# A fourth part by seven products in ten quads, and split first tiles at two stage starts, in an fp32 decoder layer on one core

## The chip, the core and the metric

The kernel runs on one core of a Trainium2 chip. Its metric is the device time of one execution in microseconds, weights in HBM at the start and the result in HBM at the end. Four engines work beside each other, each through its own list of instructions: TensorE (PE in the profile) multiplies, VectorE (DVE) and ScalarE (ACT) work elementwise, SyncE's queue (SP) issues the loads. Two elementwise engines prepare what TensorE multiplies, and semaphores make one engine wait for another.

## The reference

One layer with 256 tokens of width 2048, all in fp32 (shortened):

```python
x = x + 0.5 * swiglu(rms_norm(x, g1), w_gate1, w_up1, w_down1)     # FFN1, 2048 -> 5632 -> 2048
h = rms_norm(x, g_mix); p = h @ w_in                                # 2048 -> 5120: mixing
x = x + concat(diff_attention(q, k, v), conv_group(c_val, c_gate)) @ w_out
x = x + cross_attention(rms_norm(x, g_x), rms_norm(mem, g_mem))     # 256 memory tokens
x = x + 0.5 * swiglu(rms_norm(x, g2), w_gate2, w_up2, w_down2)      # FFN2
# swiglu(h, g, u, d) = (silu(h @ g) * (h @ u)) @ d
```

Three quarters of the time go into the two FFNs.

## The kernel before

**Splitting.** TensorE multiplies fp32 numbers in a shorter format (fp32r). So each weight tile `raw` is split in two: ACT casts it to `wh`, VectorE subtracts, `wl = raw - wh` (`split`). The activations stand turned, as `h` and `l` (`xh`, `xl`; `hth`, `htl` for the hidden layer). A product takes three matmuls of 128x128 by 512: `h*wh + h*wl + l*wh`.

**Quads.** An FFN goes through the 5632 hidden columns in 11 groups of 512, c = 0 to 10. For each, a *quad* (`quad`) computes gate and up for both token halves, four accumulators `acc[tb][j]` in PSUM (tb: token half; j: gate or up). After the groups 0 to 3, 4 to 7 and 8 to 10 two down quads follow, which add half their result to x. The weights of a quad come in 8 *parts*, one for each pair of row tiles. A plain part is 8 products, 24 matmuls, and two splits of 1024 elements per partition. A *seven* computes the same 2x2 block product by seven products instead of eight, in Winograd's way: sums of weight tiles (lines 241, 243, 244, on VectorE), sums of the tokens (`token_sums`, once per pair), 21 matmuls, and splits of 1024, 512, 1024, 1024. Some of the seven products go into tiles of their own (`q`: p1, q6, q57); after the last seven `middle` combines them (`us`, `vw`, `ys`), and at the quad's end `evac` adds the accumulators to these (lines 442), takes silu and multiplies (`h`, line 447). `S_IN` says which of the 8 pairs are sevens, `ORDER_IN` in which order the parts come; `ORDER_1` is that of FFN2's first quad, `ORDER_0` that of FFN1's first, which has no sevens.

**Order of the work.** A scheduler of the framework places the instructions of every engine; an engine goes through its list in order. The weights run through 3 buffers for `raw` and 7 each for `wh` and `wl`, so VectorE can be some parts ahead of TensorE and no more. The four accumulators have one buffer each: a quad's first matmul into one waits until the quad before it was evacuated. `later(n, fn)` postpones small work by n parts, above all the transposes of a finished tile (`turn`, 8 transposes) and the row sums.

**Stage starts.** Mixing (`proj` on `w_in`, columns 8 and 6 first) and FFN2 take x as FFN1 and cross attention leave it. x is normed by scaling behind the multiplication, so transposes of x can start at once; `after_x` sets them.

Of the kernel before, what the change touches and what calls it, by code (L numbers as in the profile page):

```python
# [52 lines left out]
def hybrid_layer(ctx, tc, x, head, xT, mem, memT, pos, convw, bvec, w):  # L53
# [16 lines left out]
    def later(steps, fn):  # L70
        waiting.append([steps, fn])
# [126 lines left out]

    def quad(parts, srcs, middle, evac, first=False):

# [4 lines left out]

        acc = [[accp.tile([P, 512], F32, tag=f"acc{tb}{j}", name=f"acc{tb}{j}") for j in range(2)]
               for tb in range(2)]
        begun = set()
# [87 lines left out]
    def token_sums(pool, bufs, o0, e0, o1, e1):  # L296
# [92 lines left out]
    class LazyStats:  # L389
        def __init__(self, norm):  # L390
            self.norm = norm

        def __len__(self):
            return KD

        def __getitem__(self, k):
            h, l = self.norm.grp[k // 4] if self.norm.grp[k // 4] else (None, None)
            return (h, l, k % 4, k)

    def after_x(norm, tb, n):  # L400

        norm.sq(tb, n)
        if tb == 1:
            later((1, 2, 2, 3)[n], lambda: norm.turn(n))
            if n == 3:
                later(3, norm.finish)


    def ffn(norm, wg, wu, wd, groups, done):
        with tc.tile_pool(name="wf", bufs=SPLITS, reuse_waits="tile") as wf, \  # L410
# [8 lines left out]
            for gi, ng in enumerate(groups):  # L419
                hts, hsums, hold = {}, {}, {}  # L420
                s_down = S_DOWN[ng]
                for c in range(c0, c0 + ng):
                    hts[c] = (hp.tile([P, 4, 256], F32R, tag="hth", name="hth"),
                              hp.tile([P, 4, 256], F32R, tag="htl", name="htl"))
                    start = norm is n1 and c == 0
                    sevens = () if start else S_IN
                    order = ORDER_0 if start else ORDER_1 if c == 0 else ORDER_IN
                    rest = {}
# [8 lines left out]
                    def evac(tb, acc, c=c, rest=rest, end=(c == c0 + ng - 1), pairs=(c - c0 < s_down)):  # L437
# [12 lines left out]
                        def turn():  # L450
# [15 lines left out]
                        later(2 if end else 8, turn)  # L466

                    quad(norm.parts(order, sevens),
                         [wg[:, c * 512:(c + 1) * 512], wu[:, c * 512:(c + 1) * 512]], middle, evac, first=start)
                final = gi == len(groups) - 1  # L470
                for n0 in (0, 2):
                    def middle(q, n0=n0):
# [6 lines left out]
                    def evac(tb, acc, n0=n0):  # L479
                        for j in range(2):  # L480
# [97 lines left out]
    def constants_b():  # L578
# [106 lines left out]

    w_in, w_out, w_kv = w["w_in"], w["w_out"], w["xattn_w_kv"]

    def wcols(wt, c):
        return wt[:, c * 512:(c + 1) * 512]

    n3 = Norm(G_XATT, "xa")
    with tc.tile_pool(name="mix", bufs=1, reuse_waits="tile") as mp:
        uT = [mp.tile([P, 4, 30 + 256], F32, name=f"uT{c}") for c in range(2)]
        y = mp.tile([P, 8, 256], F32, name="y")
        vt = [[mp.tile([P, 512], F32, name=f"v{tb}{c}") for c in range(2)] for tb in range(2)]
        for c in range(2):
# [4 lines left out]
        for c in range(2):  # L701
            def evac(tb, acc, c=c):
# [413 lines left out]
```

## Time and profile before

| | us |
|---|---|
| Median of 3 runs (lowest, highest) | 1873.14 (1871.94, 1873.90) |
| Profiled execution, its own time | 1874.74 |
| Its span on the core | 1871.8 |
| Mean granted clock of TensorE, share of 2.4 GHz | 0.998 |
| TensorE busy in the span | 1852.2 |
| VectorE busy in the span | 1676.7 |

The profiled execution is one of its own, 1.6 us above the median; all durations come from it. The time beside the span (2.9 us) lies before and after the instructions. A busy TensorE is one with a matmul in its pipe; how fast they follow one another is read from their starts.

### The profile page before, as it was taken

Reading aid. Unit: us, or ns where it says so; the run is one execution under the profiler, and the core shown is the slowest. Engines: PE = TensorE matmul, PEld = TensorE weight load, DVE = VectorE, ACT = ScalarE, POOL = GpSimd, SP = SyncE. Lnnn points to the kernel's source line nnn. Section 1 sums busy time; section 2 is a strip of 40 time slices with the busy share of each in tenths; the row PEclk is TensorE's granted clock in tenths of the full one; section 3 lists DMA queues with packets and bytes.
Section 4 is the critical chain, followed back from the end, with each engine's and each line's share of the span. In section 5 each row is a group of like instructions: output and inputs, shape, how many; then the busy total and the mean of one; then the engine's idle time right before and its main releaser. Section 6 shows DMA issues by size and latency. Waiting matters only on the chain.

```text
span 1871.8 us, 23348 instructions
## 1 busy us (share of the span) xinstructions
PE 1852.2 (99%) x8365; PEld 1524.5 (81%) x8365; DVE 1676.7 (90%) x2240; ACT 1090.6 (58%) x1470; POOL 21.7 (1%) x29
## 2 busy tenths in 40 slices
PE   9999999999999999999999999999999999999998
PEld 6878888888888887888778887888888888888887
DVE  7899999999999996799997666999999999999998
ACT  7565555565545665554577656665655556555553
POOL 0000000000000000000011000000000000000000
PEclk9999999999999999999999999999999999999999
DMA  9556556656665546766644751556655666546554
GB/s 336 199 193 203 180 176 214 212 187 200 205 222 181 202 158 209 230 206 198 178 134 129 256 182 57 203 180 215 207 191 197 227 212 203 191 157 225 186 201 153
DMA packets 188756, 364.72 MB, mean 195 GB/s; under 512 B 11616, under 2 KB 12128, under 8 KB 188640
## 3 DMA queue, kind: packets, MB, share of 16 engines
q1 hardware_dynamic: 188640, 363.23, 58.6%
q8 instruction: 65, 1.06, 0.2%
q14 instruction: 51, 0.42, 0.1%
HBM read 361.09 MB, written 2.10 MB: 194 GB/s over the span
## 4 chain that ended last, share of the span: by engine, by line
PE 71%; DVE 19%; DMA 3%; issue 3%; ACT 3%; POOL 0%; SPq 0%; DVEq 0%; ACTq 0%
PE acc L277 13%; PE acc L281 13%; PE acc L279 13%; DVE wl L146 8%; DVE y L917 4%; PE acc L182 4%; PE acc L181 4%; PE acc L184 4%; PE acc L196 3%; PE q L196 3%; PE q L197 3%; PE acc L197 3%; PE q L195 3%; PE acc L195 3%; DMA raw<-ffn_w_up 2%
## 5 line engine op out<-in xcount | busy, mean ns | idle before, releaser
L145 ACT CAST wh<-raw 128x1024 fp32r<-128x1024 f32 (+1 forms) x864 | 838.3, 1001 | 664.2 <-DVE raw L241 267.0
L146 DVE TENSOR_TENSOR wl<-raw,wh 128x1024 fp32r<-128x1024 f32 (+1 forms) x864 | 975.9, 1158 | 139.6 <-ACT wh L145 124.2
L277 PE MATMUL acc<-wh,xh_f 128*128 128x512 f32 x904 | 352.7, 393 | 6.5 <-ACT wh L145 3.6
L279 PE MATMUL acc<-wl,xh_f 128*128 128x512 f32 x904 | 351.6, 391 | 0.0
L281 PE MATMUL acc<-wh,xl_f 128*128 128x512 f32 x904 | 294.4, 390 | 0.0
L277 PEld LDWEIGHTS acc<-wh,xh_f 128*128 128x128 f32 x904 | 169.7, 188 | 45.9 <-ACT wh L145 6.0
L279 PEld LDWEIGHTS acc<-wl,xh_f 128*128 128x128 f32 x904 | 170.1, 188 | 36.5 <-DVE wl L146 2.0
L281 PEld LDWEIGHTS acc<-wh,xl_f 128*128 128x128 f32 x904 | 170.0, 188 | 35.5
L277 PE MATMUL acc<-wh,hth 128*128 128x512 f32 x448 | 174.7, 392 | 0.7 <-DVE vw L442 0.4
L279 PE MATMUL acc<-wl,hth 128*128 128x512 f32 x448 | 174.5, 390 | 0.0
L281 PE MATMUL acc<-wh,htl 128*128 128x512 f32 x448 | 147.9, 390 | 0.0
L181 PE MATMUL acc<-wh,xh_mix 128*128 128x512 f32 x320 | 125.6, 394 | 1.8 <-ACT wh L145 1.8
L182 PE MATMUL acc<-wl,xh_mix 128*128 128x512 f32 x320 | 125.3, 392 | 0.5 <-DVE wl L146 0.5
L241 DVE TENSOR_TENSOR raw<-raw 128x1024 f32<-128x1024 f32 x95 | 115.5, 1216 | 0.0
L196 PE MATMUL q<-wl,sh 128*128 128x512 f32 x285 | 110.9, 389 | 0.0
L197 PE MATMUL q<-wh,sl 128*128 128x512 f32 x285 | 110.9, 389 | 0.0
L195 PE MATMUL q<-wh,sh 128*128 128x512 f32 x285 | 110.9, 389 | 0.0
L184 PE MATMUL acc<-wh,xl_mix 128*128 128x512 f32 x320 | 102.9, 391 | 0.0
L917 DVE SCALAR_TENSOR_TENSOR y<-uT,cw,y 128x256 f32<-128x256 f32 x240 | 100.4, 470 | 0.1
L277 PEld LDWEIGHTS acc<-wh,hth 128*128 128x128 f32 x448 | 84.1, 188 | 19.7 <-DVE vw L442 1.3
L281 PEld LDWEIGHTS acc<-wh,htl 128*128 128x128 f32 x448 | 84.1, 188 | 17.6
L279 PEld LDWEIGHTS acc<-wl,hth 128*128 128x128 f32 x448 | 84.2, 188 | 16.9
(299 smaller groups left out, 2502.7 us busy)
## 6 DMA issues: line engine op xcount, KB each, us to landing
raw<-ffn_w_down SPq DMA_DIRECT2D x176, 512.0 KB, 4.8
raw<-ffn_w_gate SPq DMA_DIRECT2D x175, 512.0 KB, 4.0
raw<-ffn_w_up SPq DMA_DIRECT2D x175, 512.0 KB, 5.2
raw<-w_in SPq DMA_DIRECT2D x80, 512.0 KB, 4.4
raw<-w_out SPq DMA_DIRECT2D x32, 512.0 KB, 4.8
raw<-xattn_w_kv SPq DMA_DIRECT2D x16, 512.0 KB, 3.9
raw<-xattn_w_q SPq DMA_DIRECT2D x8, 512.0 KB, 4.3
raw<-xattn_w_o SPq DMA_DIRECT2D x8, 512.0 KB, 3.8
```

What stands on the lines that cost most here:

```text
L145: last[:] = [S.copy(out=wh, in_=raw), V.tensor_tensor(out=wl, in0=raw, in1=wh.bitcast(F32), op=ALU.subtract)]
L146: V.tensor_tensor(out=wl, in0=raw, in1=wh.bitcast(F32), op=ALU.subtract)]
L181: T.matmul(acc[tb][j], hs, wt[k, j][0], start=(fresh and k == 0), stop=False)
L182: T.matmul(acc[tb][j], hs, wt[k, j][1], start=False, stop=False)
L184: T.matmul(acc[tb][j], ls, wt[k, j][0], start=False, stop=(ending and k == nk - 1))
L195: T.matmul(acc, hs, w[0], start=start, stop=False)
L196: T.matmul(acc, hs, w[1], start=False, stop=False)
L197: T.matmul(acc, ls, w[0], start=False, stop=stop)
L277: T.matmul(acc[tb][j], hs, wt[b][j][0], start=f"{tb}{j}" not in begun, stop=False)
L279: T.matmul(acc[tb][j], hs, wt[b][j][1], start=False, stop=False)
L281: T.matmul(acc[tb][j], ls, wt[b][j][0], start=False, stop=(ending and b == 1))
L917: V.scalar_tensor_tensor(out=yc, in0=u[:, j:j + 256], scalar=cw[:, j * 8 + ct:j * 8 + ct + 1], in1=yc, op0=ALU.mult, op1=ALU.add)
```

## The change

1. In the gate/up quads with odd c of both FFNs, ten in all, four parts are sevens (pairs 1, 3, 5, 6, in the order 0, 1, 3, 2, 5, 6, 4, 7) instead of three (1, 3, 5, in order). The token sums of pair 6 are computed once per FFN for that.
2. FFN2's first quad has its three sevens at pairs 1, 5, 6 (order 0, 2, 3, 1, 4, 5, 6, 7) instead of 1, 3, 5 (order 0, 2, 1, 4, 3, 6, 5, 7).
3. `Lead`: the first pair of row tiles of mixing and of FFN2 is loaded and split while the last part of the quad or projection before it runs ("ending"), and its 24 matmuls stand right behind that, ahead of the last transposes of x.
4. Down quads that are not the last of their FFN keep their combined sevens and add them to x after the accumulators were evacuated, instead of in `middle`.
5. Smaller: token sums keep both halves in one tile (`shl`), with 4 buffers instead of 3; two tiles of mixing move into them; some transposes of x come a part later.

```diff
-ORDER_1 = (0, 2, 1, 4, 3, 6, 5, 7)
+S_1, ORDER_1 = (1, 5, 6), (0, 2, 3, 1, 4, 5, 6, 7)
+S_MORE, ORDER_MORE = (1, 3, 5, 6), (0, 1, 3, 2, 5, 6, 4, 7)
...
+    class Lead:
+        def split(self, tiles):
+            self.w = []
+            for src, (raw, wh, wl) in zip(self.srcs, tiles):
+                nc.sync.dma_start(out=raw, in_=rows_pair(src, 0))
+                split(raw, wh, wl)
+                self.w.append((wh, wl))
+
+        def multiply(self):
...
+            for tb in range(2):
+                for k in range(2):
+                    h, l, i, _ = self.stats[k]
+                    hs, ls = [t[:, i, tb * P:(tb + 1) * P] for t in (h, l)]
+                    for j in range(2):
+                        wh, wl = [t[:, k, :] for t in self.w[j]]
+                        T.matmul(acc[tb][j], hs, wh, start=(k == 0), stop=False)
+                        T.matmul(acc[tb][j], hs, wl, start=False, stop=False)
+                    for j in range(2):
+                        T.matmul(acc[tb][j], ls, self.w[j][0][:, k, :], start=False, stop=False)
...
                 ending = n == len(parts) - 1
+                if ending and ahead:
+                    ahead()
...
-                    sevens = () if start else S_IN
-                    order = ORDER_0 if start else ORDER_1 if c == 0 else ORDER_IN
+                    more = c % 2 == 1
+                    sevens = () if start else S_1 if c == 0 else S_MORE if more else S_IN
+                    order = ORDER_0 if start else ORDER_1 if c == 0 else ORDER_MORE if more else ORDER_IN
...
+                        if not final:
+                            y = fp.tile([P, 512], F32, tag="y", name="ys", bufs=1)
+                            V.tensor_tensor(out=y, in0=vw[:, 0, :], in1=q["q57"][:, 1, :], op=ALU.add)
+                            rest[:] = [(0, 0, p1, 0.5), (0, 1, vw[:, 0, :], 0.5), (1, 0, vw[:, 1, :], -0.5),
+                                       (1, 1, y, 0.5)]
+                            return
...
+                        if tb:
+                            for b, j, t, f in rest:
+                                xt = X[b][n0 + j]
+                                V.scalar_tensor_tensor(out=xt, in0=t, scalar=f, in1=xt, op0=ALU.mult, op1=ALU.add)
...
+            if c == 0:
+                proj(ks.after(2), [wcols(w_in, 8), wcols(w_in, 6)], evac, acc=open_acc)
...
+        lead = Lead(n4.stats(), [wcols(w["ffn2_w_gate"], 0), wcols(w["ffn2_w_up"], 0)])
         for n0 in (0, 2):
-            proj(xst, [wcols(w["xattn_w_o"], n0), wcols(w["xattn_w_o"], n0 + 1)], add_x2(n0))
+            proj(xst, [wcols(w["xattn_w_o"], n0), wcols(w["xattn_w_o"], n0 + 1)], add_x2(n0),
+                 ahead=n0 == 2 and (lambda: lead.split([weight_tiles() for _ in range(2)])))
+        open_acc = lead.multiply()
```

How the lists of instructions move is seen at three places. First TensorE where FFN1 ends and mixing begins, before: the last products of the down quad (`hth`, `htl`), the transposes of x, mixing (`xh_mix`).

```order
L279 MATMUL acc_5782<-wl,hth 128x512
L281 MATMUL acc_5782<-wh,htl 128x512
L329 MATMUL tp<-ident,x_75 128x128 x2
L329 MATMUL tp<-ident,x_79 128x128
L329 MATMUL tp<-ident,x_75 128x128
L329 MATMUL tp<-ident,x_79 128x128 x2
L329 MATMUL tp<-ident,x_75 128x128
L329 MATMUL tp<-ident,x_79 128x128
L181 MATMUL acc_6092<-wh,xh_mix_5759 128x512
```

And after:

```order
L316 MATMUL acc_5826<-wl,hth 128x512
L318 MATMUL acc_5826<-wh,htl 128x512
L218 MATMUL acc_6110<-wh,xh_mix_5803 128x512
L219 MATMUL acc_6110<-wl,xh_mix_5803 128x512
L218 MATMUL acc_6111<-wh,xh_mix_5803 128x512
L219 MATMUL acc_6111<-wl,xh_mix_5803 128x512
L221 MATMUL acc_6110<-wh,xl_mix_5804 128x512
```

The transposes (now line 366) have moved behind 24 matmuls of mixing, of which the first five stand here.

Second VectorE where quad 2 of FFN1 follows quad 1, before. The splits are those of quad 2's parts; `p1s`, `vw`, `ys` from `acc` are the evacuations of quad 1; `ang`, `rp_kl` and the ropes are the rotary tables.

```order
L146 TENSOR_TENSOR wl<-raw,wh 128x1024
L624 TENSOR_SCALAR rp_kl<-ang 128x16
L146 TENSOR_TENSOR wl<-raw,wh 128x512
L625 TENSOR_TENSOR rp_kl<-rp_kl,ang 128x16
L636 SCALAR_TENSOR_TENSOR ropeB<-rp_sn,small 128x8 x2
L626 TENSOR_SCALAR rp_kl<-rp_kl 128x16
L636 SCALAR_TENSOR_TENSOR ropeB<-rp_sn,small 128x8 x6
L456 TENSOR_TENSOR htl<-tp,hth 128x4x128
L634 TENSOR_TENSOR ropeA<-rp_cs,small 128x8 x8
L456 TENSOR_TENSOR htl<-tp,hth 128x4x128
L442 TENSOR_TENSOR p1s<-acc_552,p1s 128x512
```

And after, from the last evacuations on:

```order
L490 SCALAR_TENSOR_TENSOR h<-vw,rstd_f_491,p1s 128x512
L339 TENSOR_TENSOR sraw<-hold,sraw 128x128
L485 TENSOR_TENSOR vw<-acc_551,vw 128x512
L485 TENSOR_TENSOR ys<-acc_552,ys 128x512
L343 TENSOR_TENSOR shl<-sraw,shl 128x512
L490 SCALAR_TENSOR_TENSOR h<-ys,rstd_f_491,vw 128x512
L148 TENSOR_TENSOR wl<-raw,wh 128x1024 x2
L148 TENSOR_TENSOR wl<-raw,wh 128x512
```

The second split of quad 2's first part and the first two of its seven (the x2 and the 512 here) have moved from ahead of the evacuations to behind them; one split (not shown) still stands ahead.

Third VectorE where quad 1 of FFN2 follows quad 0, before; the last two of the six splits are those of quad 1's first part.

```order
L146 TENSOR_TENSOR wl<-raw,wh 128x1024 x6
L291 TENSOR_TENSOR us<-q_10358,p1s 128x512
L293 TENSOR_TENSOR vw<-q_10359,us 128x1024
L442 TENSOR_TENSOR p1s<-acc_10204,p1s 128x512
L433 TENSOR_TENSOR ys<-vw,q_10359 128x512
L442 TENSOR_TENSOR vw<-acc_10206,vw 128x512
L442 TENSOR_TENSOR vw<-acc_10205,vw 128x512
L442 TENSOR_TENSOR ys<-acc_10207,ys 128x512
L447 SCALAR_TENSOR_TENSOR h<-vw,rstd_f_10333,p1s 128x512
L447 SCALAR_TENSOR_TENSOR h<-ys,rstd_f_10333,vw 128x512
L146 TENSOR_TENSOR wl<-raw,wh 128x1024
```

And after:

```order
L148 TENSOR_TENSOR wl<-raw,wh 128x1024
L330 TENSOR_TENSOR vw<-q_10445,us 128x1024
L485 TENSOR_TENSOR p1s<-acc_10232,p1s 128x512
L476 TENSOR_TENSOR ys<-vw,q_10445 128x512
L485 TENSOR_TENSOR vw<-acc_10234,vw 128x512
L485 TENSOR_TENSOR vw<-acc_10233,vw 128x512
L485 TENSOR_TENSOR ys<-acc_10235,ys 128x512
L490 SCALAR_TENSOR_TENSOR h<-vw,rstd_f_10384,p1s 128x512
L490 SCALAR_TENSOR_TENSOR h<-ys,rstd_f_10384,vw 128x512
L148 TENSOR_TENSOR wl<-raw,wh 128x1024 x3
```

The two splits of quad 1's first part have moved behind the evacuations (they are the first two of the three in the last row).

## Rows read from the trace of the kernel before

**Rows 1.** The page, part 1: busy us (share of the span) and instructions.
```profile
PE 1852.2 (99%) x8365; PEld 1524.5 (81%) x8365; DVE 1676.7 (90%) x2240; ACT 1090.6 (58%) x1470; POOL 21.7 (1%) x29
```

**Rows 2.** Windows by quad: length, busy time of PE, PEld, DVE, ACT, POOL, granted clock, DMA.
```profile
53.83:96.94 43.11, 42.57 (x193) 35.03 (x191) 42.03 (x109) 26.04 (x33) 0.00 (x0) 1.00 0.57 196
96.94:140.72 43.78, 43.18 (x192) 35.02 (x192) 41.30 (x53) 26.86 (x33) 0.00 (x0) 1.00 0.56 192
395.54:437.94 42.40, 42.40 (x193) 35.19 (x191) 39.97 (x46) 25.67 (x30) 0.00 (x0) 1.00 0.67 224
521.82:563.40 41.58, 41.58 (x184) 34.28 (x183) 40.10 (x45) 22.70 (x25) 0.00 (x0) 1.00 0.60 202
1168.02:1211.11 43.09, 43.04 (x191) 35.11 (x192) 42.33 (x54) 29.88 (x41) 1.70 (x1) 1.00 0.61 206
1211.11:1253.68 42.57, 42.57 (x192) 35.11 (x191) 41.36 (x49) 24.84 (x31) 0.00 (x0) 1.00 0.63 212
```

**Rows 3.** Groups by line and shape, 521.82 to 648.19: busy us, mean ns, idle before.
```profile
L146 DVE TENSOR_TENSOR wl<-raw,wh 128x1024 fp32r<-128x1024 f32 x59 | 70.2, 1220 | 5.4 <-ACT wh L145 4.0
...
L241 DVE TENSOR_TENSOR raw<-raw 128x1024 f32<-128x1024 f32 x9 | 10.9, 1216 | 0.0
...
L243 DVE TENSOR_TENSOR raw<-raw 128x512 f32<-128x512 f32 x9 | 6.2, 689 | 0.2
...
L146 DVE TENSOR_TENSOR wl<-raw,wh 128x512 fp32r<-128x512 f32 x8 | 5.5, 683 | 0.0
```

**Rows 4.** Timeline of PE where FFN1 ends and mixing begins: start, duration, [idle before].
```profile
713.31 0.39 PE L281 MATMUL acc<-wh,htl 128*128 128x512 f32 x1
...
714.50 0.87 PE L329 MATMUL tp<-ident,x 128*128 128x128 f32 x6 [0.58 <-DVE x L482]
717.22 0.73 PE L181 MATMUL acc<-wh,xh_mix 128*128 128x512 f32 x2 [1.85 <-ACT wh L145]
...
724.95 0.39 PE L181 MATMUL acc<-wh,xh_mix 128*128 128x512 f32 x1
```

**Rows 5.** Windows behind the start of mixing, and in mixing (columns of rows 2).
```profile
720.00:721.00 1.00, 1.00 (x4) 0.81 (x3) 1.00 (x2) 1.00 (x2) 0.00 (x0) 0.50 0.80 274
926.00:928.00 2.00, 0.59 (x4) 0.20 (x2) 2.00 (x8) 1.25 (x3) 0.00 (x0) 1.00 0.74 192
```

**Rows 6.** Timeline of PE at the start of FFN2.
```profile
1165.91 1.03 PE L329 MATMUL tp<-ident,x 128*128 128x128 f32 x8
1168.02 1.21 PE L277 MATMUL acc<-wh,xh_f 128*128 128x512 f32 x4 [1.07 <-ACT wh L145]
```

**Rows 7.** Waits of PE behind a down quad and in FFN2's quad 3.
```profile
270.05 0.50 PE L277 MATMUL acc<-wh,xh_f 128*128 128x512 f32 x1 [0.71 <-DVE x L482]
...
1297.67 0.50 PE L277 MATMUL acc<-wh,xh_f 128*128 128x512 f32 x1 [0.98 <-DVE vw L442]
```

**Rows 8.** Timeline of DVE and of PE in FFN1's quad 1, first seven.
```profile
57.63 2.48 DVE L146 TENSOR_TENSOR wl<-raw,wh 128x1024 fp32r<-128x1024 f32 x2
...
60.69 1.23 DVE L146 TENSOR_TENSOR wl<-raw,wh 128x1024 fp32r<-128x1024 f32 x1
...
62.90 0.39 PE L196 MATMUL acc<-wl,xh_f 128*128 128x512 f32 x1
```

**Rows 9.** Timeline of DVE and of PE where FFN1's quad 2 begins.
```profile
96.71 0.28 DVE L299 TENSOR_TENSOR sraw<-hold 128x128 f32<-128x128 f32 x1
...
96.94 0.47 PE L277 MATMUL acc<-wh,xh_f 128*128 128x512 f32 x1 [0.54 <-DVE p1s L442]
...
98.05 0.50 PE L277 MATMUL acc<-wh,xh_f 128*128 128x512 f32 x1 [0.41 <-DVE vw L442]
...
101.28 0.50 PE L277 MATMUL acc<-wh,xh_f 128*128 128x512 f32 x1 [0.19 <-DVE ys L442]
```

**Rows 10.** Timeline of DVE where FFN2's quad 1 begins.
```profile
1212.58 0.75 DVE L447 SCALAR_TENSOR_TENSOR h<-ys,rstd_f,vw 128x512 f32<-128x512 f32 x1
1213.24 1.82 DVE L146 TENSOR_TENSOR wl<-raw,wh 128x1024 fp32r<-128x1024 f32 x2
```

More of the change, by code (lines that the diff above doesn't have):

```diff
@@ L146, in split, with proj @@
                    V.tensor_tensor(out=wl, in0=raw, in1=wh.bitcast(F32), op=ALU.subtract)]
-    def proj(stats, srcs, evac, acc=None):
+    def proj(stats, srcs, evac, acc=None, ahead=None):
         nj = len(srcs)
@@ L197, in passes, with quad @@
         T.matmul(acc, ls, w[0], start=False, stop=stop)
[L199 to L208, printed above, removed]
+    def quad(parts, srcs, middle, evac, first=False, acc=None, ahead=None):
+        begun = {"00", "01", "10", "11"} if acc else set()
+        acc = acc or [[accp.tile([P, 512], F32, tag=f"acc{tb}{j}", name=f"acc{tb}{j}") for j in range(2)]
+                      for tb in range(2)]
         seven = [i for i, p in enumerate(parts) if p()[4]]
@@ L270, in quad @@
                 ending = n == len(parts) - 1
+                if ending and ahead:
+                    ahead()
                 wt = [[ev0, ev1], [od0, od1]]
@@ L389, in hybrid_layer, with __init__, after @@
     class LazyStats:
-        def __init__(self, norm):
-            self.norm = norm
+        def __init__(self, norm, first=0):
+            self.norm, self.first = norm, first
+        def after(self, k):
+            return LazyStats(self.norm, k)
         def __len__(self):
-            return KD
+            return KD - self.first
         def __getitem__(self, k):
+            k += self.first
             h, l = self.norm.grp[k // 4] if self.norm.grp[k // 4] else (None, None)
@@ L403, in after_x, with ffn @@
         if tb == 1:
-            later((1, 2, 2, 3)[n], lambda: norm.turn(n))
+            later(((1, 2, 3, 3) if norm.wanted else (1, 2, 3, 4) if norm is n2 else (1, 2, 2, 3))[n],
+                  lambda: norm.turn(n))
             if n == 3:
                 later(3, norm.finish)
-    def ffn(norm, wg, wu, wd, groups, done):
+    def ffn(norm, wg, wu, wd, groups, done, acc=None, follow=None):
         with tc.tile_pool(name="wf", bufs=SPLITS, reuse_waits="tile") as wf, \
@@ L485, in evac, with ahead @@
                                 done(tb, n0 + j)
+                        if tb:
+                            for b, j, t, f in rest:
+                                xt = X[b][n0 + j]
+                                V.scalar_tensor_tensor(out=xt, in0=t, scalar=f, in1=xt, op0=ALU.mult, op1=ALU.add)
                     parts = [lambda c=c0 + i // 2, a=i % 2, i=i: (*hts[c], 2 * a, c * 4 + 2 * a,
-                                                                  a == 0 and i // 2 < s_down and hsums[c])
+                                                                  a == 0 and i // 2 < s_down and hsums.get(c, True))
                              for i in ORDER_DOWN[ng]]
-                    quad(parts, [wd[:, n * 512:(n + 1) * 512] for n in (n0, n0 + 1)], middle, evac)
+                    def ahead():
+                        raw = ph["raw"].tile([P, 4, 512], F32, tag="raw", name="raw")
+                        follow.split([(raw[:, 2 * j:2 * j + 2, :], *split_tiles()) for j in range(2)])
+                    leads = final and n0 == 2 and follow
+                    quad(parts, [wd[:, n * 512:(n + 1) * 512] for n in (n0, n0 + 1)], middle, evac,
+                         ahead=ahead if leads else None)
+                    if leads:
+                        return follow.multiply()
                 c0 += ng
-    n1 = Norm(G_FFN1, "f1", S_IN)
+    n1 = Norm(G_FFN1, "f1", S_MORE)
     n1.grp = [(xtp.tile([P, 4, 256], F32R, tag="xh", name=f"xh_f1{n}"),
@@ L642, in hybrid_layer @@
     n2 = Norm(G_MIX, "mix")
-    ffn(n1, w["ffn1_w_gate"], w["ffn1_w_up"], w["ffn1_w_down"], (4, 4, 3),
-        lambda tb, n: after_x(n2, tb, n))
+    w_in = w["w_in"]
+    open_acc = ffn(n1, w["ffn1_w_gate"], w["ffn1_w_up"], w["ffn1_w_down"], (4, 4, 3),
+                   lambda tb, n: after_x(n2, tb, n),
+                   follow=Lead(n2.stats(), [w_in[:, c * 512:(c + 1) * 512] for c in (8, 6)]))
     mids = ctx.enter_context(ExitStack())
@@ L694, in hybrid_layer @@
         y = mp.tile([P, 8, 256], F32, name="y")
-        vt = [[mp.tile([P, 512], F32, name=f"v{tb}{c}") for c in range(2)] for tb in range(2)]
+        v0 = xsp.tile([P, 2, 512], F32, tag="shl", name="v0", bufs=len(S_MORE))
+        vt = [[v0[:, c, :] for c in range(2)], [mp.tile([P, 512], F32, name=f"v1{c}") for c in range(2)]]
         for c in range(2):
```

35 lines of the change are left out of this document (24 added, 11 removed).

## The prediction

> **What bounds the kernel now.** The page first: TensorE is busy 99% of the span, VectorE 90% [rows 1]. So the end is set by TensorE wherever VectorE keeps ahead of it, and only work taken from TensorE, or a wait of TensorE, moves the time; but VectorE has a tenth to spare, and not everywhere. The windows by quad show where [rows 2]. The eighth gate/up quad of FFN1 (c = 7) lasts 42.40 us and VectorE works 39.97 of them: 2.43 idle. The next one, behind a down quad, leaves it 1.48 (41.58 - 40.10). But the second quad of the kernel (c = 1) leaves it 1.08 of 43.11, because rotary angles and small constants are made there, and the second quad of FFN2 leaves 1.21 of 42.57. From the quad at 521.82, which holds 183 matmuls and no transposes, one matmul costs TensorE 41.58 / 183 = 0.227 us; the 8 transposes of the others cost 42.40 - 41.58 = 0.82.
>
> A part of a quad gives TensorE 24 x 0.227 = 5.45 us (plain) or 21 x 0.227 = 4.77 (seven products). It costs VectorE 2 x 1.22 = 2.44 us (plain) or, by the groups of lines, 3 x 1.22 + 0.68 for the splits, 1.22 + 2 x 0.69 for the sums, 6.94 in all [rows 3]. So a seven in place of a plain part takes 0.68 us from TensorE and puts 4.50 on VectorE. Each fits only because plain parts between sevens give VectorE 3.0 us back (5.45 - 2.44).
>
> **What the change removes.** Ten quads get one seven more: 30 matmuls x 0.227 = 6.8 us.
>
> The last matmul of FFN1 starts at 713.31, eight transposes of x follow, and the first of mixing comes at 717.22, behind a wait for ACT's cast of the weights [rows 4]. Then the granted clock is down to 0.50 for some us, as in the window from 720, that is 1.2 GHz instead of 2.4 [rows 5]. The 25th matmul of mixing starts at 724.95 [rows 4]; 24 matmuls and 8 transposes would take 5.45 + 0.82 + 0.23 = 6.5 from 713.31, so 5.1 us are lost there. Afterwards 24 matmuls, whose weights are split while FFN1's last part runs, stand right behind it. They cover 5.45 us, and the next weights, which take the place of today's first (ready at 717.2), are wanted at 713.5 + 5.45 + 0.82 = 719.8. I take **-4.8** (-3.0 to -5.1, if some wait stays). At the start of FFN2 the same gap is smaller: the transposes start at 1165.91, the first matmul at 1168.02 [rows 6]; 2.11 - 0.82 = 1.3 us lost.
>
> The x-updates that down quads postpone: at 270.05 TensorE waits 0.71 us for one of them [rows 7]. I take **-0.5** (0 to -1.1) for this one place.
>
> **What it adds, place by place.** The sums go by the order of the instructions, with durations from the trace.
>
> *FFN1, quads 1 and 2.* Today TensorE first uses the last split of the first seven at 62.90, five matmuls before that part ends at 64.03; VectorE had it ready at about 60.0 and, after 0.66 us of small constants, starts the next splits at 60.69 [rows 8]: a lead of 2.9 us. Now the order is plain, seven, seven, plain, seven, seven, plain, plain. The third part's splits of sums are ready at 60.69 + 1.22 + 0.68 + 2.60 + 1.22, with 0.2 for angles 66.6; TensorE, which begins that part at 64.03, wants the first of the two at 66.3, ten matmuls on: 0.35 late. Then a plain part, and the next seven's come at about 77.9 (the row sums of the seventh pair, four of 0.28 that overlap a little [rows 9] and one as wide as the 0.69 of rows 3, stand before them) where 76.9 is wanted: 1.0. The seven right behind it is wanted 4.77 after, ready about 7.2 after: 2.5. Sum 3.9. At the quad's end VectorE's order puts the evacuations ahead of the second split of the next quad, where three splits stood ahead before. Today TensorE waits there for the evacuations, 0.54 + 0.41 + 0.19 [rows 9]; then it waits for that split, 0.69 + 0.68 + 0.69 + 1.22 behind its last matmul less 7 matmuls' cover: about 1.8. Net 0.7. With 0.7 for the three matmuls less: **+3.9** (0 to +8; VectorE alone gives +2.3 from its 5.9 us more against 1.08 + 2.48 idle in the two quads [rows 2], +5.9 if it keeps the idle time).
>
> *FFN1, quad 3.* It starts with VectorE ahead again; one short wait is left: **-0.3** (-0.8 to +1.2).
>
> *FFN2, quad 0.* Its sevens now come late, so VectorE is ahead when they do: the start's 1.3 and what the quad loses now (43.09 against the 42.40 of a late one [rows 2]), **-2.0** (-0.5 to -2.5).
>
> *FFN2, quad 1.* Before, both splits of its first part stand ahead of the evacuations; now they stand behind them. VectorE ends those today at 1213.3, with 1213.24 as the next start, and TensorE's quad begins at 1211.11 [rows 10]. The first split would be ready at 1214.5; five matmuls that need only casts cover 1.1: a wait of 2.2. From there VectorE works without a break: the first seven's sums 0.65 late, the second's, right behind, 1.95, the fourth's 1.2. Together 6.0, less 0.2 lost now (42.57 against 42.40) and 0.7 for the matmuls: **+5.1** (+1 to +7).
>
> *FFN2, quads 2 and 3.* One split behind the evacuations again, 0.69 + 0.68 + 1.22 against 1.6 of cover: **+1.0** (0 to +1.5). Quad 3 loses 0.98 today to an evacuation [rows 7]; that goes, with 0.7 of matmuls, and some 0.8 comes back from its sevens: **-0.9** (-2.1 to +0.8).
>
> *The other six odd quads.* Two quads have 2.43 + 1.48 idle at least, and are asked for 4.50 + 0.68. VectorE's lead there is large at the start of each quad (up to the 7 split buffers), so I count 0.3 of waits per quad: 6 x (-0.68 + 0.3) = **-2.3** (-4.1 to +1).
>
> Transfers cost nothing: the loads are the same, the queue of SP only takes the first two of mixing and FFN2 earlier, under 5.45 us of matmuls; uncovered, they would cost what the lead gains. ACT's casts, one and a half more per odd quad, lie in the idle half of its time (22.70 busy of 41.58 [rows 2]).
>
> **The sum.** -4.8 - 0.5 + 3.9 - 0.3 - 2.0 + 5.1 + 1.0 - 0.9 - 2.3 = -0.8 us. It is made against the profiled run, 1874.74; the median of the runs is 1873.14, 1.6 lower, so **1872.3** is forecast. The ends of all ranges add up to -14.7 and +16.0, but do not come together.
>
> A rule bears on that. VectorE takes the split behind the evacuations only after them, as rows 10 show (the split starts when they end). The Trainium skill ("TensorE: Matmul & The Clock Gate", architectural detail of the array) says that VectorE's and ScalarE's queues are strict FIFO. By that the waits of 2.2 and 1.8 stand as counted, and the trace agrees; an engine that took what is ready would save about 4 us, for a sum near -4.8.
>
> **Rivals.** (a) *VectorE absorbs it.* For it: 7 split buffers let it run ahead, and matmuls that need only casts can fill its lateness, as at several places today. With the waits of the two second quads halved (2.3 and 3.0) and none in the quads behind them, -0.8 - 2.3 - 3.0 - 1.0 - 0.8 = -7.9: 1865.2. Against it: the idle time of rows 2 is smaller than what is asked for. (b) *The clock falls in the new waits*, the slower case. A wait of 1.85 us before mixing was followed by half clock, and 5.1 were lost there, 3.2 more than waited [rows 4, 5]; in 926 to 928 TensorE was idle for 2.00 - 0.59 = 1.41 and the clock stayed at 1.00 [rows 5]. Three of the waits above (2.5, 2.2, 1.95) lie near. If each comes in one piece and is long enough, 3 x 3.2 = +9.6: 1881.9. It decides whether a new wait turns out like the first of these two or like the second. Against it: casts alone let TensorE go on between. The Trainium skill (same page, the HAM clock gate) says that the clock is 1.2 GHz by default and that activity releases it, so an idle stretch takes it back; it would give this case, and the trace so far shows both. (c) *The lead does nothing*: its successors come late, the wait moves behind the 24 matmuls with its half clock, and +4.8 + 0.5 gives 1877.6. Against it: today's weights are there 2.6 us before they would be wanted.
>
> **How the numbers follow.** About 0.2% (3.7 us) is what measuring can tell from no change. Likeliest, 0.46: the sum, with its own range of 1868 to 1876. Rival (a) 0.28, at 1860 to 1868. (b) 0.13, (c) 0.13. Faster by over 0.2% (under 1869.4) is (a) and a quarter of the first, 0.40; slower (over 1876.9) is (b) and nearly all of (c), 0.24; the rest 0.36. The range, 1863 to 1880, leaves out the end of (a) and the worse half of (b).
>
> **What would show it.** TensorE runs through into 24 matmuls of mixing with clock 1.00 at 714 to 724; the quads at 53.8 and at FFN2's second place last 45 to 47.5 us, with waits for wl at the sevens that follow sevens; the late odd quads last 41.7 to 42.1 us. Wrong it is if the second quads end in 43 us or less, if quads behind them lose what I give them, or if the clock falls inside an FFN.

## The result: 1.3% slower

| | median us (lowest to highest), runs | ratio to before, 95% interval |
|---|---|---|
| before | 1872.56 (1871.94 to 1873.90), 4 | |
| changed | 1897.18 (1896.10 to 1898.02), 4 | 1.0130 (1.0113 to 1.0148) |

24.6 us more, outside the range. The page of the changed kernel, to be read beside [rows 1]; the last line is the head of part 4, the chain that ended last:

```profile
span 1896.2 us, 23356 instructions
...
PE 1860.2 (98%) x8335; PEld 1519.7 (80%) x8335; DVE 1717.4 (91%) x2300; ACT 1096.1 (58%) x1496; POOL 20.4 (1%) x29
...
PE 40%; DVE 37%; DMA 8%; ACT 7%; issue 6%; SPq 1%; POOL 0%; ACTq 0%; DVEq 0%
```

TensorE does 30 matmuls less (x8335) and is longer under way all the same. VectorE works 1717.4 us, 40.7 more than before; on the chain that ended last it holds 37%, and TensorE only 40%. The same line of the page before:

```profile
PE 71%; DVE 19%; DMA 3%; issue 3%; ACT 3%; POOL 0%; SPq 0%; DVEq 0%; ACTq 0%
```

The stage starts did what was forecast. Timeline of TensorE where FFN1 ends, against [rows 4]:

```profile
729.53 0.39 PE L318 MATMUL acc<-wh,htl 128*128 128x512 f32 x1
729.76 0.39 PE L218 MATMUL acc<-wh,xh_mix 128*128 128x512 f32 x1
...
735.20 1.03 PE L366 MATMUL tp<-ident,x 128*128 128x128 f32 x8
735.99 0.71 PE L185 MATMUL acc<-wh,xh_mix 128*128 128x512 f32 x2
```

The 25th matmul of mixing comes 6.46 us behind FFN1's last (735.99 - 729.53), where it was 11.64. At FFN2 the same distance is 6.46 for 8.25. So 5.2 and 1.8 us were won.

The quads lost more than that. Windows by quad (columns as in [rows 2]): quads 1 and 2 of FFN1; c = 5, 6, 7; c = 10 and the first down quad behind it; quads 1, 2 and 3 of FFN2:

```profile
54.02:101.51 47.49, 44.66 (x189) 35.53 (x188) 44.46 (x100) 28.15 (x36) 0.00 (x0) 0.96 0.47 155
101.51:149.82 48.31, 44.68 (x193) 35.94 (x191) 45.19 (x69) 26.99 (x34) 0.00 (x0) 0.96 0.58 196
320.87:362.57 41.70, 41.70 (x189) 34.62 (x188) 40.81 (x47) 24.80 (x31) 0.00 (x0) 1.00 0.59 196
362.57:405.88 43.31, 43.01 (x193) 35.03 (x191) 41.78 (x50) 25.15 (x31) 0.00 (x0) 1.00 0.59 200
405.88:449.30 43.42, 42.57 (x190) 34.39 (x188) 41.98 (x52) 26.04 (x32) 0.00 (x0) 1.00 0.55 186
617.72:662.04 44.32, 42.61 (x192) 34.95 (x191) 40.89 (x46) 25.53 (x31) 0.00 (x0) 1.00 0.61 201
662.04:696.73 34.69, 34.27 (x148) 27.96 (x149) 31.45 (x39) 20.09 (x25) 0.00 (x0) 0.95 0.54 178
1223.26:1270.22 46.96, 44.76 (x190) 35.49 (x188) 44.53 (x52) 26.90 (x34) 0.00 (x0) 0.96 0.56 186
1270.22:1315.00 44.78, 43.25 (x192) 34.94 (x191) 43.77 (x53) 25.41 (x31) 0.00 (x0) 1.00 0.62 211
1315.00:1359.17 44.17, 42.63 (x189) 34.46 (x188) 41.51 (x49) 26.61 (x33) 0.00 (x0) 1.00 0.52 172
```

The same quads of before, as far as [rows 2] don't show them: quad 3 of FFN1; c = 5, 6, 10 and the first down quad behind; quads 2 and 3 of FFN2:

```profile
140.72:183.55 42.83, 42.55 (x192) 35.02 (x191) 40.55 (x46) 24.99 (x31) 0.00 (x0) 1.00 0.62 209
310.78:353.15 42.37, 42.37 (x192) 35.19 (x191) 39.50 (x48) 25.64 (x30) 0.00 (x0) 1.00 0.59 199
353.15:395.54 42.39, 42.39 (x193) 35.19 (x191) 40.34 (x49) 25.49 (x31) 0.00 (x0) 1.00 0.59 198
605.79:648.19 42.40, 42.40 (x192) 35.19 (x191) 40.21 (x48) 25.68 (x30) 0.00 (x0) 1.00 0.66 223
648.19:680.50 32.31, 32.31 (x149) 26.82 (x148) 29.52 (x35) 19.04 (x24) 0.00 (x0) 1.00 0.54 175
1253.68:1296.07 42.39, 42.39 (x192) 35.19 (x191) 38.92 (x46) 24.31 (x30) 0.00 (x0) 1.00 0.59 198
1296.07:1339.79 43.72, 42.73 (x192) 35.11 (x191) 41.23 (x49) 26.16 (x31) 0.00 (x0) 1.00 0.61 208
```

The two set against each other, in us:

| place | forecast | measured |
|---|---|---|
| start of mixing | -4.8 | -5.2 |
| FFN1, quads 1 and 2 | +3.9 | +4.4 and +4.5 |
| FFN1, quad 3 | -0.3 | +1.7 |
| quad behind FFN1's first down quads | -0.5 | -0.2 |
| start of FFN2 and its quad 0 | -2.0 | +0.2 (-1.8 + 2.0) |
| FFN2, quad 1 | +5.1 | +4.4 |
| FFN2, quad 2 | +1.0 | +2.4 |
| FFN2, quad 3 | -0.9 | +0.5 |
| the six later odd quads themselves | -2.3 | 0.0 |
| all other quads, gate/up and down (those behind c = 5, 7, 9: +11.5) | none | +10.5 |
| FFN1's first quad, the middle of mixing | none | +1.1 |
| sum | -0.8 | +24.3 |

The largest line is one that the forecast didn't have. The quad with c = 5 does give its 0.68 (41.70 for 42.37); but the one behind it, which the change doesn't touch, lasts 43.31 where it was 42.39, and so it goes on. In that quad (c = 6) the lead of VectorE is gone at the first seven; timelines of VectorE and of TensorE:

```profile
365.34 0.69 DVE L485 TENSOR_TENSOR ys<-acc,ys 128x512 f32<-128x512 f32 x1
365.94 0.69 DVE L148 TENSOR_TENSOR wl<-raw,wh 128x512 fp32r<-128x512 f32 x1
...
369.80 5.91 DVE L148 TENSOR_TENSOR wl<-raw,wh 128x1024 fp32r<-128x1024 f32 x5
```

```profile
371.07 0.50 PE L231 MATMUL q<-wl,shl 128*128 128x512 f32 x1
```

The split that begins at 369.80 ends at about 371.0, and TensorE uses it at 371.07 ([rows 8] show a lead of 2.9 in the worst quad of before). Ahead of it on VectorE stand the evacuations of the quad before, the last at 365.34, 2.8 us behind that quad's end, and the sums.

Splits are the smaller part of what TensorE waits for in the late quads, though. Its waits from c = 5 to the end of FFN1 (us in total, times, longest):

```profile
PE acc L314 <- DVE p1s L485: 1.7, 1, 1.7
PE acc L314 <- DVE vw L485: 1.0, 3, 0.4
PE q L231 <- DVE wl L148: 0.5, 1, 0.5
```

With two short ones (0.4 and 0.2) that is 3.3 us for evacuations and x-updates at the quads' passages and 0.5 for splits; in FFN2 from c = 4 on it is 3.1 and 0.5. Before, the same view lists no wait in either stretch. So a late VectorE mostly shows where one quad hands its accumulators to the next.

The longest of these waits, 1.71 us behind c = 10, begins with a late load. SyncE's queue, ACT and VectorE there:

```profile
645.13 0.65 SPq L263 DMA_DIRECT2D raw<-ffn_w_down  x1
...
651.52 2.00 ACT L147 CAST wh<-raw 128x1024 fp32r<-128x1024 f32 x2 [3.81 <-DMA raw<-ffn_w_down]
...
652.61 1.22 DVE L148 TENSOR_TENSOR wl<-raw,wh 128x1024 fp32r<-128x1024 f32 x1 [2.77 <-ACT wh L147]
```

VectorE frees the `raw` buffers in bunches: three parts are issued at 644.72, 646.99 and 649.26, 2.3 us apart, where they were 2.7 to 3.4 apart before. ACT waits 3.81 us for the first, VectorE 2.77 us for ACT, and then works without a break up to the evacuation that TensorE waits for. With the half clock behind it, c = 10 and the down quad lose 4.3 us here.

At the passage from quad 1 to quad 2 of FFN1, timelines of TensorE, VectorE and ACT:

```profile
103.33 0.39 PE L230 MATMUL p<-wh,xh_f 128*128 128x512 f32 x1
106.54 0.50 PE L314 MATMUL acc<-wh,xh_f 128*128 128x512 f32 x1 [2.83 <-DVE vw L485]
```

```profile
101.23 0.63 DVE L703 SCALAR_TENSOR_TENSOR ropeB<-rp_sn,small 128x8 f32<-128x8 f32 x7 [0.47 <-ACT rp_sn L690]
103.63 0.71 DVE L701 TENSOR_TENSOR ropeA<-rp_cs,small 128x8 f32<-128x8 f32 x8 [1.77 <-ACT rp_cs L694]
...
105.80 0.69 DVE L485 TENSOR_TENSOR vw<-acc,vw 128x512 f32<-128x512 f32 x1
```

```profile
99.68 1.28 ACT L690 ACT_TABLE_LOAD   x1
...
101.47 1.28 ACT L488 ACT_TABLE_LOAD   x1
...
103.40 0.20 ACT L694 ACTIVATE rp_cs<-rp_kl 128x16 f32<-128x16 f32 x1
```

TensorE waits 2.83 us for an accumulator that `vw` at 105.80 must free. VectorE stands ahead of that in `ropeA`, 1.77 us, for the cosines, which ACT makes at 103.40 behind a second table load (1.28 us each). Before, VectorE didn't wait there, and the same eight `ropeA` stood ahead of the first evacuation (96.11):

```profile
94.90 0.69 DVE L634 TENSOR_TENSOR ropeA<-rp_cs,small 128x8 f32<-128x8 f32 x8
```

The wait of 2.83 us was followed by half clock, and so was one of 1.71 us at 662.04, behind c = 10. Windows:

```profile
105.00:107.00 2.00, 0.46 (x2) 0.41 (x3) 2.00 (x6) 1.08 (x2) 0.00 (x0) 1.00 0.00 0
107.00:109.00 2.00, 2.00 (x7) 1.58 (x6) 2.00 (x4) 0.25 (x1) 0.00 (x0) 0.58 0.00 0
663.00:667.00 4.00, 3.84 (x10) 3.06 (x11) 4.00 (x9) 1.52 (x3) 0.00 (x0) 0.58 0.17 64
```

From 107 to 109 and from 663 to 667 the granted clock is 0.58 of 2.4 GHz, that is mostly the lower of the two levels, 1.2 GHz.

### The profile page after: what moved, and what is told of

The parts are those of the page before. It is cut to its first block, busy times and chain, and to the rows that moved or that the text cites. A ratio compares the mean times of both kernels' runs of the same rounds, so it can differ in the third digit from the quotient of the medians.

```text
span 1896.2 us, 23356 instructions
## 1 busy us (share of the span) xinstructions
PE 1860.2 (98%) x8335; PEld 1519.7 (80%) x8335; DVE 1717.4 (91%) x2300; ACT 1096.1 (58%) x1496; POOL 20.4 (1%) x29
## 4 chain that ended last, share of the span: by engine, by line
PE 40%; DVE 37%; DMA 8%; ACT 7%; issue 6%; SPq 1%; POOL 0%; ACTq 0%; DVEq 0%
DVE wl L148 16%; PE acc L318 6%; PE acc L316 6%; PE acc L314 6%; ACT wh L147 6%; DMA raw<-ffn_w_up 5%; DVE y L992 4%; DVE raw L276 4%; PE acc L185 4%; PE acc L188 4%; PE acc L186 4%; DMA raw<-ffn_w_down 3%; DVE raw L279 2%; DVE raw L278 2%; PE q L231 1%
## 5 line engine op out<-in xcount | busy, mean ns | idle before, releaser
L148 DVE TENSOR_TENSOR wl<-raw,wh 128x1024 fp32r<-128x1024 f32 (+1 forms) x884 | 988.2, 1156 | 119.8 <-ACT wh L147 110.4
L314 PE MATMUL acc<-wh,xh_f 128*128 128x512 f32 x816 | 318.9, 395 | 8.3 <-DVE vw L485 4.2
L316 PE MATMUL acc<-wl,xh_f 128*128 128x512 f32 x816 | 318.2, 393 | 1.0 <-DVE wl L148 1.0
L318 PE MATMUL acc<-wh,xl_f 128*128 128x512 f32 x816 | 267.5, 391 | 0.0
L314 PEld LDWEIGHTS acc<-wh,xh_f 128*128 128x128 f32 x816 | 154.0, 189 | 45.4 <-DVE vw L485 6.3
L316 PEld LDWEIGHTS acc<-wl,xh_f 128*128 128x128 f32 x816 | 154.1, 189 | 34.9 <-DVE wl L148 3.9
L318 PEld LDWEIGHTS acc<-wh,xl_f 128*128 128x128 f32 x816 | 154.5, 189 | 32.6
L276 DVE TENSOR_TENSOR raw<-raw 128x1024 f32<-128x1024 f32 x105 | 128.0, 1219 | 0.0
L231 PE MATMUL q<-wl,shl 128*128 128x512 f32 x315 | 124.2, 394 | 2.1 <-DVE wl L148 1.9
L230 PE MATMUL q<-wh,shl 128*128 128x512 f32 x315 | 123.5, 392 | 1.6 <-ACT wh L147 1.5
L232 PE MATMUL q<-wh,shl 128*128 128x512 f32 x315 | 123.3, 391 | 0.0
```

The lines of the kernel that those rows point to most:

```text
L148: V.tensor_tensor(out=wl, in0=raw, in1=wh.bitcast(F32), op=ALU.subtract)]
L230: T.matmul(acc, hs, w[0], start=start, stop=False)
L231: T.matmul(acc, hs, w[1], start=False, stop=False)
L276: V.tensor_tensor(out=raw[:, 1:3, :], in0=raw[:, 1:3, :], in1=raw[:, 2:4, :], op=ALU.add)
L314: T.matmul(acc[tb][j], hs, wt[b][j][0], start=f"{tb}{j}" not in begun, stop=False)
L316: T.matmul(acc[tb][j], hs, wt[b][j][1], start=False, stop=False)
```

## Experiments

Theory A: VectorE's time is the cause. The fourth seven makes its splits late, and what is late then is the split of the next quad. Theory B: the other edits have moved evacuations ahead of splits. All times are medians in us; every ratio is to the kernel before on the same chip. The medians of before on these chips lie between 1870.2 and 1872.6, so a difference of two medians can be off by some 2 us (load7x, by the ratios, lies 22 us over no_fourth and not 20).

| kernel | median | ratio (95%) |
|---|---|---|
| no_fourth | 1868.48 | 0.9979 (0.9971 to 0.9988) |
| only_fourth | 1898.76 | 1.0141 (1.0127 to 1.0155) |
| only_lead | 1869.72 | 0.9988 (0.9979 to 0.9997) |
| alternate | 1886.76 | 1.0081 (1.0068 to 1.0095) |
| late_only | 1880.96 | 1.0053 (1.0039 to 1.0067) |
| ropes_late | 1890.74 | 1.0099 (1.0083 to 1.0114) |
| load7 | 1887.28 | 1.0084 (1.0070 to 1.0097) |
| load7x | 1888.76 | 1.0098 (1.0081 to 1.0115) |
| load3 | 1878.68 | 1.0034 (1.0022 to 1.0047) |
| pool_sums | 1971.16 | 1.0531 (1.0518 to 1.0545) |
| mix_lead | 1866.53 | 0.9971 (0.9960 to 0.9983) |
| mix_lead_ropes | 1863.42 | 0.9953 (0.9940 to 0.9966) |

**no_fourth**: three sevens in the odd quads, all other edits kept.

```diff
-                    more = c % 2 == 1
+                    more = False
-    n1 = Norm(G_FFN1, "f1", S_MORE)
+    n1 = Norm(G_FFN1, "f1", S_IN)
```

> The changed kernel with three sevens in the odd quads again, the rest of the change kept. Theory A (the fourth seven makes VectorE late and its whole order of splits and evacuations with it): the two stage starts keep their 5.2 and 1.8 us and the time is about 1865.5. Theory B (the other parts, above all the postponed x-updates and the later transposes, have pushed the evacuations ahead of the splits): most of the loss stays, over 1885.

1868.5: B falls as the cause of the whole. The fourth seven is worth 1897.2 - 1868.5 = +28.7 us, although it takes 6.8 us of matmuls away. The starts' 7 us are not all kept: from cross attention's last matmul to FFN2's quad 2 it takes 4.1 us more than before (1159.9 to 1252.0, where it was 1165.7 to 1253.7). There B holds: FFN2's quad 0 loses 2.0 us as in the changed kernel, and its quad 1, with three sevens, still lasts 46.46 where it was 42.57 (46.96 in the changed kernel), half clock included:

```profile
1205.52:1251.98 46.46, 44.90 (x193) 36.23 (x191) 44.84 (x53) 27.00 (x34) 0.00 (x0) 0.96 0.62 211
```

**only_fourth**: the change without `Lead`, with the old first quad of FFN2, old down quads and old steps.

```diff
-S_1, ORDER_1 = (1, 5, 6), (0, 2, 3, 1, 4, 5, 6, 7)
+S_1, ORDER_1 = (1, 3, 5), (0, 2, 1, 4, 3, 6, 5, 7)
-                        if not final:
+                        if False:
-                   follow=Lead(n2.stats(), [w_in[:, c * 512:(c + 1) * 512] for c in (8, 6)]))
+                   follow=None)
```

> The ten quads with a fourth seven alone; stage starts, FFN2's first quad and the down quads as before. Theory A: the loss without the 7 us that the starts give, about 1902 (1897 to 1906). Theory B: 1866 to 1876.

1898.8, the other side of the same split: A holds in that the fourth seven is the cause. That the split is what comes late is only part of it, by the waits above.

**only_lead**: the split first tiles and the later steps alone: no_fourth with the first two edits of only_fourth.

> The split first tiles at the two stage starts and the later transposes alone. Both theories: 5.2 + 1.8 us less than before, 1865.5; if the following parts give it back, 1870 or more.

1869.7, 4 us over the forecast. Timeline of TensorE in its first quad of FFN2:

```profile
1176.05 0.47 PE L230 MATMUL p<-wh,xh_f 128*128 128x512 f32 x1 [0.49 <-DVE xl_f L370]
...
1179.23 0.79 PE L230 MATMUL acc<-wh,xh_f 128*128 128x512 f32 x1 [2.25 <-ACT wh L147]
```

It starts earlier and then waits for the first seven, whose sums and token sums VectorE makes no sooner.

**alternate**: the same ten quads with `ORDER_MORE = (1, 0, 3, 2, 5, 4, 6, 7)`, seven, plain, seven, plain.

> The changed kernel with the order seven, plain, seven, plain and so on in the odd quads: the same work on every engine. Theory A1 (the loss comes from sevens that stand next to each other, 2 us of lead each): about 1875 to 1882. Theory A2 (VectorE's whole time in a pair of quads is too small, or the order at the quads' ends): 1892 to 1900.

1886.8 is between the two: 10.4 us are won where no seven stands behind a seven, 18.3 over no_fourth remain. Neither A1 nor A2 alone; and this order also puts a seven first, behind the evacuations, where quad 1 of FFN2 loses 6.6 us instead of 4.4.

**late_only**: `more = c % 2 == 1 and c > 3`.

> The changed kernel with the fourth seven only in c = 5, 7, 9 (both FFNs), so 18 matmuls less than no_fourth instead of 30. From the trace of the changed kernel its late quads lose 10 us by themselves; if that is their own doing, the time is no_fourth + 8 to 11 = 1877 to 1880. If it was only carried over from the late starts, the 18 matmuls show: 1864.4.

1881.0, 12.5 over no_fourth with six of the ten quads. By the windows 8.2 us of it lie in c = 5 and the quads from there to each FFN's end, as expected: the late quads lose by themselves, where [rows 2] show 2.43 us idle in c = 7. Another 4.3 lie in quad 2 of FFN1, though quad 1 has no fourth seven here, only the token sums of pair 6; c = 0 gives 1.8 back. VectorE at the passage from quad 1 to quad 2:

```profile
96.60 0.71 DVE L701 TENSOR_TENSOR ropeA<-rp_cs,small 128x8 f32<-128x8 f32 x8 [1.97 <-ACT rp_cs L694]
```

The tables stand between the evacuations again, and quad 2 loses as much against before (+4.4) as in the changed kernel, with three sevens in quad 1.

**load7** and **load7x**: no_fourth with the load alone, in the odd quads.

```diff
+                if loaded and n in (4, 6):
+                    t = stat.tile([P, 512], BF16, tag="junk", name="junk", bufs=1)
+                    for i in range(4 if n == 4 else 3):
+                        V.tensor_tensor(out=t, in0=raw[:, 0, :], in1=raw[:, 1, :], op=ALU.add)
```

The sum is thrown away, and nothing reads it. load7x reads `X[0][0]` and `X[0][1]` instead of `raw`. load3 has `n == 4` and three adds.

> no_fourth with seven more adds of 512 elements on VectorE (4.8 us, results unused) in each odd quad, behind two of its plain parts: VectorE's load of the fourth seven without its matmuls, buffers and order of parts. If VectorE's time is the cause, about the loss of the fourth seven less its 0.68 per quad: no_fourth + 15 to 30, 1884 to 1898. If it is the order of the parts and the evacuations, within 4 us of no_fourth.

> load7 with the seven unused adds reading two tiles of x instead of the weight tile, so that they hold no load buffer: only VectorE's time is left of the fourth seven. If that time is the cause, as in load7: no_fourth + 14 to 20, 1883 to 1888. If load7 lost by loads that started later, most of it goes: under 1876.

1887.3 and 1888.8: 18.8 and 20.3 over no_fourth, for 70 x 0.69 = 48 us of VectorE. So a load of about the fourth seven's size, with no other order of parts, costs two thirds of what the fourth seven costs. Where it lies, by the windows of c = 5, 6, 7 and the down quad behind them in load7:

```profile
312.72:355.10 42.38, 42.38 (x193) 35.17 (x191) 41.45 (x51) 23.26 (x29) 0.00 (x0) 1.00 0.58 199
355.10:397.96 42.86, 42.68 (x193) 35.11 (x191) 40.00 (x48) 24.70 (x30) 0.00 (x0) 1.00 0.57 196
397.96:441.53 43.57, 42.86 (x192) 34.96 (x191) 42.14 (x51) 24.73 (x30) 0.00 (x0) 1.00 0.56 188
441.53:484.21 42.68, 42.68 (x192) 35.04 (x192) 40.53 (x48) 25.17 (x31) 0.00 (x0) 1.00 0.63 206
```

The loaded quad c = 5 (312.72) loses nothing, the unloaded one behind it 0.5, the second loaded one 1.2, the down quad 0.3: the pattern of the changed kernel. In load7x the scheduler drew the adds forward, into quads ahead of the odd ones; there, and not in c = 5, 7, 9, lie its losses. So it doesn't repeat load7 at the same places, and it puts the load of two quads into one stretch (14 adds in FFN2's quad 0, +5.4); but the adds hold no load buffer and cost as much.

**load3**

> no_fourth with three unused adds of 512 (2.1 us of VectorE) in each odd quad, where seven of them cost 18.8 us in all. If VectorE had spare time that the seven used up first, the first three are nearly free: no_fourth + 0 to 4, 1868 to 1873. If every microsecond on VectorE costs alike, 3/7 of 18.8: no_fourth + 8, about 1876.5.

1878.7, 10.2 over no_fourth for 2.1 us per odd quad. The first microseconds are not free, as idle time of 2.4 would suggest. Whether it is more than 3/7 of load7 (8.1) its six runs, from 1874.2 to 1882.5, don't tell. In its trace, which is of the slowest of them, 7.0 of 12.3 us lie in c = 7 and the down quad behind it (2.4 each in FFN1, 1.5 and 0.8 in FFN2); in FFN1 VectorE waits 2.0 us there for a cast behind a late load, as in the changed kernel behind c = 10. These adds read `raw` and hold its buffer, so the loads' share and VectorE's are not separated here.

**ropes_late**: the tables and constants 23 parts later.

```diff
-    later(10, lambda: behind_last(constants_a))
-    later(11, lambda: behind_last(constants_b))
+    later(33, lambda: behind_last(constants_a))
+    later(34, lambda: behind_last(constants_b))
```

> The changed kernel with the rotary tables and small constants made in the first down quad instead of in FFN1's second quad. If they are what made quads 1 and 2 of FFN1 lose 8.9 us (the two table loads of ACT stand in VectorE's way ahead of the evacuations), 4 to 6 us less than the changed kernel: 1891 to 1893. If the fourth seven alone is enough there, within 1.5 us of 1897.

1890.7, 6.4 less than the changed kernel. By the windows quads 1 and 2 of FFN1 lose 1.9 instead of 8.9; the down quads that make the tables now lose 4.1, where they had won 0.5. So tables and constants were the larger part of that loss; moved to the down quads they cost less, but not nothing.

**pool_sums**: in the odd quads the two 512-wide sums on GpSimd.

```diff
-                V.tensor_tensor(out=raw[:, 3, :], in0=raw[:, 3, :], in1=raw[:, 1, :], op=ALU.add)
-                V.tensor_tensor(out=raw[:, 0, :], in0=raw[:, 0, :], in1=raw[:, 3, :], op=ALU.add)
+                E = G if loaded else V
+                E.tensor_tensor(out=raw[:, 3, :], in0=raw[:, 3, :], in1=raw[:, 1, :], op=ALU.add)
+                E.tensor_tensor(out=raw[:, 0, :], in0=raw[:, 0, :], in1=raw[:, 3, :], op=ALU.add)
```

> The changed kernel with the two 512-wide sums of each seven in the odd quads (8 per quad, 5.5 us of VectorE) on GpSimd, which is idle there; same parts, same order, same splits. If VectorE's time is the cause and GpSimd answers in about 1 us, most of the loss goes: 1870 to 1880. If GpSimd takes several us for an add, or takes VectorE's port with it, the sums themselves come late: over 1897.

1971.2: the second case, and far over it. Groups by line on GpSimd, columns as in [rows 3]:

```profile
L280 POOL TENSOR_TENSOR raw<-raw 128x512 f32<-128x512 f32 x40 | 82.6, 2064 | 3.1
L279 POOL TENSOR_TENSOR raw<-raw 128x512 f32<-128x512 f32 x40 | 52.6, 1314 | 1077.1 <-DVE raw L276 641.8 <-DMA raw<-ffn_w_gate 297.2 <-issue 103.2
```

The two adds take 1.3 and 2.1 us behind one another, 3.4 instead of 1.4, and the splits of these sums come late with them. By the waits of VectorE from 54 to 700 us it stands 67.1 us before splits whose casts are not there, where it was 20.1 in the changed kernel and 26.2 before. It says nothing against A, and nothing for it: the chain got longer while the load got smaller.

**mix_lead** and **mix_lead_ropes**: of the change only `Lead` at mixing and the postponed x-updates (only_lead without the second `Lead`, with `if not final`), then the tables in the down quad as well.

> Of the change only the split first tiles of mixing and the postponed x-updates; FFN2's start, its first quad and all sevens as before. no_fourth gained 5 us at mixing and lost most of FFN2's gain again in FFN2's first quad, so 1872.6 - 5.2 - 1.0 = 1866.4; if FFN2's first quad gives back mixing's gain too, 1868 to 1870.

> mix_lead with the rotary tables made in the first down quad. The three-seven quads 1 and 2 lose 1.6 us in the kernel before, mostly where evacuations and tables meet: 1 to 1.6 us less than mix_lead, 1865. If the down quad then waits for the tables, no gain.

1866.5 and 1863.4, both as forecast or better; the second is the fastest kernel here, 0.9953 of before. Its VectorE works as long as before, by the page:

```profile
span 1861.2 us, 23337 instructions
...
PE 1847.3 (99%) x8365; PEld 1523.3 (82%) x8365; DVE 1676.9 (90%) x2240; ACT 1091.5 (59%) x1470; POOL 20.9 (1%) x29
```

## Why the prediction was wrong

**Right.** The bound, the price of a seven on both engines, the start of mixing (-5.2 for -4.8), the size of FFN2's quad 1 (+4.4 for +5.1). Its cause came out only in half, and the size is luck in that part: no_fourth loses 3.9 in the same quad with three sevens that don't stand behind one another. There TensorE waits for a split (0.6) and for a cast (0.9) at the quad's start, with half clock behind; the 3.8 us that were counted for late sevens are not what makes it.

**The step that failed** is the one on the other six odd quads: "Two quads have 2.43 + 1.48 idle at least, and are asked for 4.50 + 0.68 ... so I count 0.3 of waits per quad". It took the idle time of VectorE for time to spare, and by its own figures even that was not enough: 5.18 us are asked of 3.91, so VectorE ends each such pair 1.27 us later, 7.6 us in six, which the lead was to carry. late_only and load7 show that it doesn't: with 4.5 and 4.8 us more in c = 5, TensorE doesn't wait in that quad, because the lead carries it, but VectorE is late at the passage into the next quad and at its first seven, and c = 7 already loses by itself (+0.8 and +1.2). I counted waits only in the quads that got the seven; +10.5 came in the others, above all as waits for evacuations (6.4 us for these and x-updates, 1.0 for splits), and 1.4 to 2.0 us more than forecast per place in FFN1's quad 3, FFN2's quads 2 and 3.

Why the idle time isn't spare can be read from what released the casts that VectorE waited for. Before, between 54 and 700, it waited 26.2 us for casts at 34 places: at 21 (17.1 us) the cast had waited for a matmul that freed a split buffer, so VectorE was as far ahead as the buffers let it; at 10 (6.5 us) for a load. In the changed kernel it is 20.1 us at 20 places: 3.1 for matmuls, 12.8 at 11 places for loads. load7 puts 24 us of adds into the same stretch, and these waits shrink by 7.1 only, from 26.2 in no_fourth to 19.1.

**A term put at nothing: the loads.** "Transfers cost nothing: the loads are the same". The loads are the same, but a late VectorE frees their buffers late and in bunches, and behind c = 10 VectorE then idles 2.77 us for one of them. What this costs in all no run separates; in load7x the waits behind loads don't grow (4.0 us in FFN1, 6.5 in no_fourth) and the loss is there all the same, so it is not the only way.

**Mis-sized: FFN1, quads 1 and 2**, +8.9 for +3.9. The forecast had VectorE's order at the passage, and the split behind the evacuations, but not that the rotary tables stand there too and that VectorE waits for ACT's table loads inside that order; ropes_late takes 7.0 of the 8.9 away from these quads, and late_only has the 4.4 of quad 2 without a fourth seven in quad 1. The four sevens without the tables cost 1.9 there, half of what was counted. **Mis-sized: FFN2's start**, +0.2 for -2.0: the gap of 1.8 closes, and the first quad loses 2.0, with a wait of 0.93 for a split at 1214.91 as the longest.

**The rivals.** (a), that VectorE absorbs it, is refuted. (b), half clock behind new waits, did occur, behind 2.83 and 1.71 us of waiting, and here as a consequence: windows of the changed kernel have a mean clock of 0.96 in quads 1 and 2 of FFN1 and quad 1 of FFN2, 0.95 behind c = 10. 0.04 of 48 us is some 2 us a quad: an estimate of at most 7 to 8 us in all, part of the lines of the table; the one in FFN2's quad 1 is in no_fourth too. (c) did not occur.

**The clock's rule and the order's rule.** The Trainium skill ("TensorE: Matmul & The Clock Gate", the HAM clock gate) has the clock fall when the engine idles and rise with activity; the trace agrees, with 0.58 in the windows behind both waits. The Trainium skill (same page, architectural detail of the array) has VectorE's queue as strict FIFO; the trace agrees, with `ropeA` at 103.63 holding up an evacuation at 105.80 whose input was there when the last matmul of quad 1 ended, at 101.7.

**Open.** The 28.7 us of the fourth seven are made up of load (about 19, load7), of sevens next to each other (10.4, alternate) and of the tables (6.4, ropes_late); these sum to 36 and so overlap, and how, no run shows. Nor does any run have more split or load buffers.

## What to carry to other kernels

Where one engine prepares what another uses through a few buffers, its idle share is not its slack: measure the slack by adding unused work of the size in question, and look for the loss in the stage behind. A saving on the bounding engine that costs its supplier 6.6 times as much (4.50 for 0.68) pays only where the supplier's lead at the tightest use stays positive through the passage into the next stage, evacuations included. And look at what shares the list with the urgent instructions: constants that could be made at any time belong where the lead is large.

## What the runs showed of the hardware

An add of 128x512 fp32 takes 0.69 us on VectorE and 1.3 to 2.1 on GpSimd. A table load of ACT takes 1.28 us, and two small activations between silus cost two of them. Behind a wait of TensorE of 1.71 us the granted clock was 0.58 for 4 us; before the change, 1.41 us idle within 2 had left it at 1.00.
